# Rotary embedding on one core: VectorE work regrouped into four operations per batch, and the tables and two rows of the first batch moved to SyncE's queue in float32

## Chip, cores and metric

The kernel runs on one core of a Trainium2 chip. The metric is the device time of one execution in microseconds (us). Several executions are taken of each kernel, and a kernel under test is always timed beside the kernel before on the same chip. In the lines from the profiler, DVE is VectorE, POOL is GpSimd, ACT is ScalarE and SPq is SyncE's queue. HBM is the chip's main memory and SBUF the core's own.

## The reference

```python
x:   (8, 2048, 16, 64) float32          # batch, position, head, feature
cos, sin: (2048, 32) float32
x1, x2 = x[..., :32], x[..., 32:]
out1 = x1 * cos - x2 * sin              # cos, sin broadcast over batch and head
out2 = x1 * sin + x2 * cos
return concatenate([out1, out2], axis=-1)   # float32
```

The input is 67.1 MB and the output is 67.1 MB. Each batch is 8.39 MB of float32. The arithmetic is six operations per pair of elements, so the work is mostly moving data.

## The kernel before

Each of the 128 partitions holds J = 16 consecutive positions of one batch: 16 rows of 1024 elements. GpSimd issues every transfer. Loads convert float32 to float16 on the way in, and stores convert back. Five batch tiles are in rotation.

```python
io_pool  = tile_pool(bufs=5)
tmp_pool = tile_pool(bufs=2)
# cos_sb, sin_sb: [P, J, 32] float16

def load(b):
    xt = io_pool.tile([P, J, H, D], f16)
    nc.gpsimd.dma_start(out=xt, in_=x[b]...)          # float32 -> float16
    return xt

def tables():
    nc.gpsimd.dma_start(out=sin_sb, in_=sin...)
    nc.gpsimd.dma_start(out=cos_sb, in_=cos...)

def rotate(xt):
    for j0 in range(0, J, 8):                         # two halves of a batch
        ...                                           # js, v1, v2, x1, x2, sin_b, cos_b
        nc.vector.tensor_mul(out=v1, in0=x2, in1=sin_b)
        nc.vector.tensor_mul(out=v2, in0=x1, in1=sin_b)
        nc.vector.tensor_mul(out=xw, in0=xw, in1=cos_b)    # both halves of the features
        nc.vector.tensor_sub(out=x1, in0=x1, in1=v1)
        nc.vector.tensor_add(out=x2, in0=x2, in1=v2)

for b in range(B):
    tiles[b] = load(b)
    if b == 0:
        tables()
    if b >= 4:
        ...                                           # store b - 4
    rotate(tiles[b])
...                                                   # the last four stores
```

GpSimd issues the transfers in this order: load 0, tables, loads 1 to 4, stores 0 and 1, loads 5 and 6, stores 2 and 3, load 7, stores 4 to 7. A load that reuses a tile waits until the store from that tile has landed.

## Time and profile before

| | before |
|---|---|
| median of the first 3 executions | 318.91 us (318.77 to 319.09) |
| span of the profiled execution | 317.2 us |
| VectorE busy | 210.7 us, 66% |
| DMA queue, share of 16 engines' span | 99.6% |
| HBM traffic | 134.7 MB, 425 GB/s |

These lines are from the page of the kernel before. The rows of digits divide the span into 40 slices and give the busy share of each in tenths. The queue line gives packets, megabytes, and the packets' time as a share of 16 DMA engines' span.

```profile
span 317.2 us, 164 instructions
DVE 210.7 (66%) x80; POOL 9.9 (3%) x22
...
DVE  0009999999999999999069999995009994000000
...
DMA  7979999999999999999999999999999999999996
...
q0 software_dynamic: 2592, 100.93, 99.6%
...
HBM read 67.63 MB, written 67.11 MB: 425 GB/s over the span
```

VectorE has empty slices at the start, in the middle and at the end. The DMA row has none. The 7s near the start are an artefact: a packet is counted in the slice in which it starts, and packets here last 2.4 us and start in bunches of 16. A queue that is 99.6% busy leaves almost nothing to gain, unless the bytes, the time of a packet or the ends of the run change.

The groups of instructions (busy time in us, then mean ns of one, then the idle time before them) give the price of a VectorE operation.

```profile
L55 DVE TENSOR_TENSOR v<-xt,sin_sb 128x4096 f16<-128x4096 f16 x16 | 36.5, 2284 | 54.2 <-DMA xt<-in_x_dram 29.9
L58 DVE TENSOR_TENSOR xt<-xt,cos_sb 128x8192 f16<-128x8192 f16 x16 | 70.7, 4416 | 0.0
```

Twice the elements cost 1.93 times as much. So an operation is nearly all streaming and has only a small fixed part.

The view of waits (total us, number of waits, longest one) shows who waits for whom.

```profile
POOL xt L37 <- DMA out_dram<-xt: 118.1, 3, 56.4
POOL out_dram L68 <- DVE xt L60: 73.8, 2, 48.0
POOL out_dram L73 <- DVE xt L60: 63.0, 2, 46.2
DVE v L55 <- DMA xt<-in_x_dram: 29.9, 2, 20.2
DVE v L55 <- DMA sin_sb<-in_sin_dram: 24.3, 1, 24.3
```

GpSimd's long waits look alarming, but an issuing engine may wait as long as the DMA queue still holds work. The order of time on GpSimd shows how early the last stores are issued.

```profile
200.67 1.05 POOL L73 DMA_DIRECT2D out_dram<-xt  x2
218.56 0.53 POOL L73 DMA_DIRECT2D out_dram<-xt  x1 [16.84 <-DVE xt L60]
265.27 0.53 POOL L73 DMA_DIRECT2D out_dram<-xt  x1 [46.18 <-DVE xt L60]
```

The last store is issued at 265.3 us. By the trace's packet records its data do not start to move until 295.4. By this reading VectorE could finish the last batch almost 30 us later without any effect (an estimate).

Last, the start, in windows of 0.25 us. The columns are the window, its length, the busy time and instructions of VectorE and of GpSimd, the granted TensorE clock, and the DMA share and GB/s. These last two again go by the start of packets, so the share can exceed 1.

```profile
2.25:2.50 0.25, 0.00 (x0) 0.25 (x2) 1.00 0.00 0
2.50:2.75 0.25, 0.00 (x0) 0.25 (x1) 1.00 4.12 655
```

The DMA engines get their first data packet at 2.61 us. From there to 315.41 us the queue never runs dry.

### The profile page before, as it was taken

To read this page: it belongs to the slowest core of one execution; us is meant where nothing else is said; L and a number is where in the kernel's file an instruction comes from. 1 tells how busy PE (TensorE), PEld (TensorE's weight loads), DVE (VectorE), ACT (ScalarE), POOL (GpSimd) and SP (SyncE) were. 2 spreads that over 40 slices of the span, in tenths; PEclk is the share of its full clock that TensorE was granted. 3 is DMA by queue.
4 is the path that set the end of the run, shared out by engine and by line. 5 is a ranking of instruction groups with operands and counts; after the bars stand their busy time and mean duration, and the time that the engine had idled before them with its cause. 6 is when DMAs were issued, how large, how long until landed. Compare 5 with 4: busy or idle time off the path is not lost.

```text
span 317.2 us, 164 instructions
## 1 busy us (share of the span) xinstructions
DVE 210.7 (66%) x80; POOL 9.9 (3%) x22
## 2 busy tenths in 40 slices
DVE  0009999999999999999069999995009994000000
POOL 5000000000000000001000000100000000000000
DMA  7979999999999999999999999999999999999996
GB/s 132 256 163 266 207 198 202 260 198 198 198 264 264 397 397 529 397 331 231 231 198 199 380 413 397 454 471 264 198 314 413 397 446 479 397 397 512 413 397 264
DMA packets 2593, 100.93 MB, mean 318 GB/s; under 512 B 288, under 2 KB 544, under 8 KB 544
## 3 DMA queue, kind: packets, MB, share of 16 engines
q0 software_dynamic: 2592, 100.93, 99.6%
q14 instruction: 1, 0.01, 0.0%
HBM read 67.63 MB, written 67.11 MB: 425 GB/s over the span
## 4 chain that ended last, share of the span: by engine, by line
issue 34%; DMA 19%; DVE 16%; another core or an unknown queue 13%; POOL 1%; POOLq 0%; DVEq 0%; PEldq 0%
DMA xt<-in_x_dram 12%; DMA sin_sb<-in_sin_dram 7%; DVE xt L58 5%; DVE v L55 3%; DVE xt L60 3%; DVE v L56 3%; DVE xt L59 2%; POOL xt L37 1%; POOL out_dram L68 1%; POOLq L101 0%; POOLq L37 0%; POOLq L73 0%; DVEq L55 0%; PEldq L101 0%
## 5 line engine op out<-in xcount | busy, mean ns | idle before, releaser
L55 DVE TENSOR_TENSOR v<-xt,sin_sb 128x4096 f16<-128x4096 f16 x16 | 36.5, 2284 | 54.2 <-DMA xt<-in_x_dram 29.9
L58 DVE TENSOR_TENSOR xt<-xt,cos_sb 128x8192 f16<-128x8192 f16 x16 | 70.7, 4416 | 0.0
L59 DVE TENSOR_TENSOR xt<-xt,v 128x4096 f16<-128x4096 f16 x16 | 36.5, 2283 | 0.1
L60 DVE TENSOR_TENSOR xt<-xt,v 128x4096 f16<-128x4096 f16 x16 | 36.5, 2283 | 0.0
L56 DVE TENSOR_TENSOR v<-xt,sin_sb 128x4096 f16<-128x4096 f16 x16 | 36.5, 2283 | 0.0
L37 POOL DMA_DIRECT2D xt<-in_x_dram x8 | 4.4, 568 | 118.9 <-DMA out_dram<-xt 118.1
L68 POOL DMA_DIRECT2D out_dram<-xt x4 | 2.1, 539 | 73.8 <-DVE xt L60 73.8
L73 POOL DMA_DIRECT2D out_dram<-xt x4 | 2.1, 532 | 63.0 <-DVE xt L60 63.0
L44 POOL DMA_DIRECT2D cos_sb<-in_cos_dram x1 | 0.5, 548 | 0.0
L43 POOL DMA_DIRECT2D sin_sb<-in_sin_dram x1 | 0.5, 542 | 0.0
L90 POOL MEMSET const-float32-0.0<- 128x1 f32 x1 | 0.1, 100 | 0.2 <-issue 0.2
L90 POOL MEMSET const-bfloat16-1.0<- 128x1 bf16 x1 | 0.1, 103 | 0.0
L90 POOL MEMSET const-float32-1.0<- 128x1 f32 x1 | 0.1, 100 | 0.0
L90 POOL MEMSET const-uint8-127<- 128x1 uint8 x1 | 0.1, 100 | 0.0
## 6 DMA issues: line engine op xcount, KB each, us to landing
xt<-in_x_dram POOLq DMA_DIRECT2D x8, 4096.0 KB, 39.8
sin_sb<-in_sin_dram POOLq DMA_DIRECT2D x1, 128.0 KB, 22.2
cos_sb<-in_cos_dram POOLq DMA_DIRECT2D x1, 128.0 KB, 22.4
out_dram<-xt POOLq DMA_DIRECT2D x8, 65.9
```

The costliest lines, as they stand in the source:

```text
L37: nc.gpsimd.dma_start(out=xt, in_=x[b].rearrange("(p j) h d -> p (j h d)", j=J))
L43: nc.gpsimd.dma_start(out=sin_sb, in_=sin.rearrange("(p j) d -> p (j d)", j=J))
L44: nc.gpsimd.dma_start(out=cos_sb, in_=cos.rearrange("(p j) d -> p (j d)", j=J))
L55: nc.vector.tensor_mul(out=v1, in0=x2, in1=sin_b)
L56: nc.vector.tensor_mul(out=v2, in0=x1, in1=sin_b)
L58: nc.vector.tensor_mul(out=xw, in0=xw, in1=cos_b)
L59: nc.vector.tensor_sub(out=x1, in0=x1, in1=v1)
L60: nc.vector.tensor_add(out=x2, in0=x2, in1=v2)
L68: nc.gpsimd.dma_start(out=out[b - 4].rearrange("(p j) h d -> p (j h d)", j=J), in_=tiles[b - 4])
L73: nc.gpsimd.dma_start(out=out[b].rearrange("(p j) h d -> p (j h d)", j=J), in_=tiles[b])
L90: nc = _bacc.Bacc("TRN2", target_bir_lowering=False, num_devices=1)
```

## The change

It has two parts. The first regroups VectorE's work: the two halves of a batch are done at once, a negated sine table turns the subtraction into an addition, and a batch takes four operations in place of ten. The second lets SyncE start the first data: both tables and two of the sixteen rows of batch 0 are loaded in float32 on its queue, and ScalarE converts them to float16. (In both kernels every transfer that converts is issued by GpSimd; SyncE's are in float32.)

```diff
+    JA = 2
+    head = const_pool.tile([P, JA, H, D], f32)
+    nc.sync.dma_start(out=head..., in_=x0[:, 0:JA, :]...)
+    nc.sync.dma_start(out=sin_f, in_=sin...)          # float32 tables
+    nc.sync.dma_start(out=cos_f, in_=cos...)
     def load(b):
+        j0 = JA if b == 0 else 0
-        nc.gpsimd.dma_start(out=xt, in_=x[b]...)
+        nc.gpsimd.dma_start(out=xt[:, j0:J, :, :]..., in_=x[b]...[:, j0:J, :]...)
-    def tables(): ...                                 # two loads on GpSimd
     def rotate(xt):
-        for j0 in range(0, J, JC): ...                # five operations per half
+        nc.vector.tensor_mul(out=v[:, :, :, 0:Dh], in0=xt[:, :, :, Dh:D], in1=neg_b)
+        nc.vector.tensor_mul(out=v[:, :, :, Dh:D], in0=xt[:, :, :, 0:Dh], in1=sin_b)
+        nc.vector.tensor_mul(out=xw, in0=xw, in1=cos_b)
+        nc.vector.tensor_add(out=xa, in0=xa, in1=v...)
+    tiles = [load(b) for b in range(NBUF)]
+    nc.scalar.copy(out=tiles[0][:, 0:JA, :, :]..., in_=head...)
+    nc.scalar.copy(out=sin_h, in_=sin_f)
+    nc.scalar.mul(out=neg_h, in_=sin_f, mul=-1.0)
+    nc.scalar.copy(out=cos_h, in_=cos_f)
     for b in range(B):
         rotate(tiles[b])
+        store(b, tiles[b])
+        if b + NBUF < B:
+            tiles.append(load(b + NBUF))
```

Cuts are marked by "...". The order in which GpSimd issues loads and stores comes out the same as before, without the tables.

More of the change, by code (lines that the diff above doesn't have):

```diff
@@ L20 @@
     f16 = mybir.dt.float16
+    f32 = mybir.dt.float32
     B, S, H, D = x.shape
@@ L25 @@
     J = S // P
-    JC = 8
+    NBUF = 5
     const_pool = ctx.enter_context(tc.tile_pool(name="rope_const", bufs=1))
-    io_pool = ctx.enter_context(tc.tile_pool(name="rope_io", bufs=5))
-    tmp_pool = ctx.enter_context(tc.tile_pool(name="rope_tmp", bufs=2))
-    cos_sb = const_pool.tile([P, J, Dh], f16)
-    sin_sb = const_pool.tile([P, J, Dh], f16)
+    io_pool = ctx.enter_context(tc.tile_pool(name="rope_io", bufs=NBUF))
+    tmp_pool = ctx.enter_context(tc.tile_pool(name="rope_tmp", bufs=1))
@@ new lines @@
+    JA = 2
+    head = const_pool.tile([P, JA, H, D], f32)
+    x0 = x[0].rearrange("(p j) h d -> p j (h d)", j=J)
+    nc.sync.dma_start(
+        out=head.rearrange("p j h d -> p (j h d)"),
+        in_=x0[:, 0:JA, :].rearrange("p j f -> p (j f)"),
+    )
+    sin_f = const_pool.tile([P, J, Dh], f32)
+    cos_f = const_pool.tile([P, J, Dh], f32)
+    cos_h = const_pool.tile([P, J, Dh], f16)
+    sin_h = const_pool.tile([P, J, Dh], f16)
+    neg_h = const_pool.tile([P, J, Dh], f16)
+    nc.sync.dma_start(out=sin_f, in_=sin.rearrange("(p j) d -> p j d", j=J))
@@ L35, in load @@
+    nc.sync.dma_start(out=cos_f, in_=cos.rearrange("(p j) d -> p j d", j=J))
     def load(b):
         xt = io_pool.tile([P, J, H, D], f16)
+        j0 = JA if b == 0 else 0
         nc.gpsimd.dma_start(
-            out=xt, in_=x[b].rearrange("(p j) h d -> p (j h d)", j=J)
-        )
-        return xt
-    def tables():
-        nc.gpsimd.dma_start(out=sin_sb, in_=sin.rearrange("(p j) d -> p (j d)", j=J))
-        nc.gpsimd.dma_start(out=cos_sb, in_=cos.rearrange("(p j) d -> p (j d)", j=J))
+            out=xt[:, j0:J, :, :].rearrange("p j h d -> p (j h d)"),
+            in_=x[b].rearrange("(p j) h d -> p j (h d)", j=J)[:, j0:J, :].rearrange("p j f -> p (j f)"),
+        )
+        return xt
@@ L46, in rotate, with store @@
+    def store(b, xt):
+        nc.gpsimd.dma_start(
+            out=out[b].rearrange("(p j) h d -> p (j h d)", j=J), in_=xt
+        )
     def rotate(xt):
-        for j0 in range(0, J, JC):
-            js = slice(j0, j0 + JC)
-            v1 = tmp_pool.tile([P, JC, H, Dh], f16)
-            v2 = tmp_pool.tile([P, JC, H, Dh], f16)
-            x1 = xt[:, js, :, 0:Dh]
-            x2 = xt[:, js, :, Dh:D]
-            sin_b = sin_sb[:, js, :].unsqueeze(2).to_broadcast([P, JC, H, Dh])
-            cos_b = cos_sb[:, js, :].unsqueeze(2).to_broadcast([P, JC, 2 * H, Dh])
-            nc.vector.tensor_mul(out=v1, in0=x2, in1=sin_b)
-            nc.vector.tensor_mul(out=v2, in0=x1, in1=sin_b)
-            xw = xt[:, js, :, :].rearrange("p j h (e d) -> p j (h e) d", d=Dh)
-            nc.vector.tensor_mul(out=xw, in0=xw, in1=cos_b)
-            nc.vector.tensor_sub(out=x1, in0=x1, in1=v1)
-            nc.vector.tensor_add(out=x2, in0=x2, in1=v2)
@@ L62 @@
-    tiles = {}
-    for b in range(B):
-        tiles[b] = load(b)
-        if b == 0:
-            tables()
-        if b >= 4:
-            nc.gpsimd.dma_start(
-                out=out[b - 4].rearrange("(p j) h d -> p (j h d)", j=J), in_=tiles[b - 4]
-            )
+        v = tmp_pool.tile([P, J, H, D], f16)
+        sin_b = sin_h.unsqueeze(2).to_broadcast([P, J, H, Dh])
+        neg_b = neg_h.unsqueeze(2).to_broadcast([P, J, H, Dh])
+        cos_b = cos_h.unsqueeze(2).to_broadcast([P, J, 2 * H, Dh])
@@ new lines, in rotate @@
+        nc.vector.tensor_mul(out=v[:, :, :, 0:Dh], in0=xt[:, :, :, Dh:D], in1=neg_b)
+        nc.vector.tensor_mul(out=v[:, :, :, Dh:D], in0=xt[:, :, :, 0:Dh], in1=sin_b)
+        xw = xt.rearrange("p j h (e d) -> p j (h e) d", d=Dh)
+        nc.vector.tensor_mul(out=xw, in0=xw, in1=cos_b)
+        xa = xt.rearrange("p j h d -> p (j h d)")
+        nc.vector.tensor_add(out=xa, in0=xa, in1=v.rearrange("p j h d -> p (j h d)"))
+    tiles = [load(b) for b in range(NBUF)]
+    nc.scalar.copy(
+        out=tiles[0][:, 0:JA, :, :].rearrange("p j h d -> p (j h d)"),
+        in_=head.rearrange("p j h d -> p (j h d)"),
+    )
@@ L71 @@
+    nc.scalar.copy(out=sin_h, in_=sin_f)
+    nc.scalar.mul(out=neg_h, in_=sin_f, mul=-1.0)
+    nc.scalar.copy(out=cos_h, in_=cos_f)
+    for b in range(B):
         rotate(tiles[b])
-    for b in range(B - 4, B):
-        nc.gpsimd.dma_start(
-            out=out[b].rearrange("(p j) h d -> p (j h d)", j=J), in_=tiles[b]
-        )
+        store(b, tiles[b])
+        if b + NBUF < B:
+            tiles.append(load(b + NBUF))
 _INS = ['x', 'cos', 'sin']
```

## The prediction

> **What bounds the kernel now.** The DMA engines. The page's queue part gives the one software queue 99.6% of 16 engines' span; VectorE is busy 210.7 of 317.2 us (66%). The trace's packet records show the first data packet at 2.6 us, the last ending at 315.4, and no gap between: eight loads and eight stores, each 128 packets (8 per engine) of about 2.43 us for 64 KB of HBM data, so 19.5 us per transfer of 8.39 MB; 16 x 19.5 = 312. HBM carries 134.7 MB at 425 GB/s. The chain of waits is no guide: it calls a third of the span "issue" because transfers queue behind each other.
>
> **What the change does.**
> - VectorE: ten operations per batch become four. From the groups, 4096 elements take 2.283 us and 8192 take 4.416, so 16384 should take 8.68 (estimate). A batch is then 2 x 4.42 + 2 x 8.68 = 26.2 us, against 26.3 now (210.7 / 8): no element is saved, only fixed cost. This assumes two elements a cycle, which the Trainium skill (VectorE: DVE Perf Modes, "The perf-mode tier table") gives as the best of a 16-bit tensor-tensor operation; the 2.283 us agree (4096 / 2 / 0.96 GHz = 2.13, plus 0.15). I expect VectorE at 207 to 210 us.
> - ScalarE: four small conversions, a few us, early, off the path.
> - DMA: HBM bytes are unchanged. Two of 16 rows of batch 0 (1 MB, some 2.4 us of all engines, estimate) and the tables (1.3 us now, between landings at 23.6 and 24.8) move to another queue, still on the same 16 engines: the Trainium skill (DMA: Bandwidth & Descriptors, "Issuing engines are not separate DMA queues") says that this saves only issue time. GpSimd issues loads and stores in the same order as before.
>
> **What lies on the critical path.** Only the start. Engines are released at 0.84 us, data flows from 2.6, and the first round of packets takes 2.9 to 3.4 us in place of 2.43. SyncE may get data moving some tenths of a us earlier and fill part of the slow first round: 0 to 1.5 us, about 0.8. The end (last store landing at 315.7, span ending 1.5 later) is unchanged.
>
> VectorE's slack hides the rest: store 0 is issued at 53 us but moves only from 102; store 7 is issued at 265 and moves from about 296. Even if SyncE's small packets take turns one for one with the 64 KB packets, so that VectorE starts at 42 instead of 24, batch 0 is ready by 69.
>
> **Prediction.** 318.1 us (before: 318.91); 8 in 10 between 316.9 and 319.2. Faster by over 2%: 0.01; within 2%: 0.98; slower by over 2%: 0.01.
>
> **What would show it right or wrong.**
> - Queue part: software queue near 98 to 99%, a new hardware queue near 1%; HBM bytes as before.
> - Groups: two operations of 4.4 and two of 8.7 us per batch. About 8.6 and 17.2 would mean the fast mode is lost: VectorE, near 410 us, would be the bound.
> - Packet records: first data at 1.8 to 2.6 us; 19.3 to 19.5 us between landings; last store landing 0 to 1.5 us earlier.
> - Stores issued before the queue runs dry.
>
> **What would make it wrong.** Two queues costing the engines efficiency while both are active (at most the first 20 to 40 us); first data no earlier; a longer launch with two more engines in use; the fast mode lost with the strided output of the sine products.

## The result and the profile after

| | before | after |
|---|---|---|
| median of 6 executions | 319.03 us (318.77 to 319.15) | 317.86 us (317.65 to 317.96) |
| ratio after / before | | 0.9963, 95% interval 0.995 to 0.9976 |
| span of the profiled execution | 317.2 us | 316.1 us |
| VectorE busy | 210.7 us | 209.2 us |
| first data packet | 2.61 us | 1.74 us |
| last data packet ends | 315.41 us | 314.27 us |

The change is worth 1.2 us, or 0.4%, and lies within 2%.

The page of the changed kernel:

```profile
span 316.1 us, 121 instructions
...
DVE 209.2 (66%) x32; ACT 4.9 (2%) x5; POOL 8.8 (3%) x20
...
DVE  0009799999999999999879999990009993000000
...
DMA  9899999999999999999999999999999999999996
...
q0 software_dynamic: 2304, 100.14, 98.5%
q1 hardware_dynamic: 432, 1.57, 1.4%
HBM read 67.63 MB, written 67.11 MB: 426 GB/s over the span
```

HBM bytes are the same to the last digit shown. A hardware queue (SyncE's) has appeared with 1.4%, and the two queues' shares add up to 99.9%. The DMA engines are as full as they were.

The groups:

```profile
L70 DVE TENSOR_TENSOR xt<-xt,cos_h 128x16384 f16<-128x16384 f16 x8 | 69.5, 8692 | 2.0 <-ACT cos_h L81 1.7
L67 DVE TENSOR_TENSOR v<-xt,neg_h 128x8192 f16<-128x8192 f16 x8 | 35.4, 4426 | 52.2 <-DMA xt<-in_x_dram 52.0
L72 DVE TENSOR_TENSOR xt<-xt,v 128x16384 f16<-128x16384 f16 x8 | 69.5, 8692 | 0.3
L68 DVE TENSOR_TENSOR v<-xt,sin_h 128x8192 f16<-128x8192 f16 x8 | 35.4, 4419 | 0.0
```

Four operations do the work of ten in the same time: 48 operations less have saved 1.5 us of VectorE's 210.7, and VectorE idles as before.

The waits:

```profile
POOL out_dram L58 <- DVE xt L72: 136.3, 4, 50.5
POOL xt L51 <- DMA out_dram<-xt: 118.3, 3, 56.4
DVE v L67 <- DMA xt<-in_x_dram: 52.0, 3, 24.8
ACT cos_h L81 <- DMA cos_f<-in_cos_dram: 17.7, 1, 17.7
...
DVE xt L70 <- ACT cos_h L81: 1.7, 1, 1.7
```

GpSimd's two sums are what they were (136.3 against 73.8 + 63.0, and 118.3 against 118.1). One new wait has come: the cosine table arrives late. The table of DMA issues (KB, then us from issue to landing) shows how late:

```profile
head<-in_x_dram SPq DMA_DIRECT2D x1, 1024.0 KB, 4.8
sin_f<-in_sin_dram SPq DMA_DIRECT2D x1, 256.0 KB, 13.4
cos_f<-in_cos_dram SPq DMA_DIRECT2D x1, 256.0 KB, 31.8
```

The tables are small, but a table packet is one row of 2 KB. The packet records suggest that each DMA engine takes about one such packet, then one 57 KB packet of batch 0 (2.13 us), and so on in turns: from 7.4 to 20.5 us, 80 table packets start in six rounds of 16 large packets. VectorE loses 1.7 us to it and has the slack to lose it.

The last stores on GpSimd:

```profile
199.55 1.05 POOL L58 DMA_DIRECT2D out_dram<-xt  x2
212.86 0.53 POOL L58 DMA_DIRECT2D out_dram<-xt  x1 [12.25 <-DVE xt L72]
263.88 0.53 POOL L58 DMA_DIRECT2D out_dram<-xt  x1 [50.50 <-DVE xt L72]
```

The last store is issued 1.4 us earlier, close to the size of the whole gain. That suggests a rival explanation, which the experiments test. The start, in the same windows (there is now a column for ScalarE):

```profile
1.50:1.75 0.25, 0.00 (x0) 0.25 (x1) 0.25 (x1) 1.00 0.51 66
1.75:2.00 0.25, 0.00 (x0) 0.25 (x1) 0.25 (x2) 1.00 1.74 295
```

Data flow from 1.74 us, which is 0.87 us earlier than before. SyncE began to issue at 0.74 us and its first packet came 1.00 us later. GpSimd began at 1.25 in both kernels, and its first packet came 1.36 us later in the kernel before. So 0.51 us is the earlier issue and 0.36 the shorter time from issue to first packet.

### The profile page after: what moved, and what is told of

Its sections match the earlier page's. It is cut to its first block, busy times and chain, and to the rows that moved or that the text cites. A ratio compares the mean times of both kernels' runs of the same rounds, so it can differ in the third digit from the quotient of the medians.

```text
span 316.1 us, 121 instructions
## 1 busy us (share of the span) xinstructions
DVE 209.2 (66%) x32; ACT 4.9 (2%) x5; POOL 8.8 (3%) x20
## 3 DMA queue, kind: packets, MB, share of 16 engines
q0 software_dynamic: 2304, 100.14, 98.5%
## 4 chain that ended last, share of the span: by engine, by line
issue 44%; DVE 14%; another core or an unknown queue 14%; DMA 10%; POOL 1%; SPq 0%; ACT 0%; POOLq 0%
DMA cos_f<-in_cos_dram 10%; DVE xt L70 6%; DVE xt L72 6%; DVE v L67 1%; DVE v L68 1%; POOL out_dram L58 1%; POOL xt L51 0%; ACT cos_h L81 0%; POOLq L112 0%; SPq L45 0%; SPq L36 0%; POOLq L58 0%
## 5 line engine op out<-in xcount | busy, mean ns | idle before, releaser
L70 DVE TENSOR_TENSOR xt<-xt,cos_h 128x16384 f16<-128x16384 f16 x8 | 69.5, 8692 | 2.0 <-ACT cos_h L81 1.7
L67 DVE TENSOR_TENSOR v<-xt,neg_h 128x8192 f16<-128x8192 f16 x8 | 35.4, 4426 | 52.2 <-DMA xt<-in_x_dram 52.0
L72 DVE TENSOR_TENSOR xt<-xt,v 128x16384 f16<-128x16384 f16 x8 | 69.5, 8692 | 0.3
L68 DVE TENSOR_TENSOR v<-xt,sin_h 128x8192 f16<-128x8192 f16 x8 | 35.4, 4419 | 0.0
L58 POOL DMA_DIRECT2D out_dram<-xt x8 | 4.3, 535 | 136.3 <-DVE xt L72 136.3
L51 POOL DMA_DIRECT2D xt<-in_x_dram x8 | 4.4, 559 | 119.1 <-DMA out_dram<-xt 118.3
L75 ACT CAST xt<-head 128x2048 f16<-128x2048 f32 x1 | 1.9, 1897 | 3.5 <-DMA head<-in_x_dram 3.5
## 6 DMA issues: line engine op xcount, KB each, us to landing
cos_f<-in_cos_dram SPq DMA_DIRECT2D x1, 256.0 KB, 31.8
```

Source lines behind the costliest of these rows:

```text
L51: nc.gpsimd.dma_start(out=xt[:, j0:J, :, :].rearrange("p j h d -> p (j h d)"), in_=x[b].rearrange("(p j) h d -> p j (h d)", j=J)[:, j0:J, ...
L58: nc.gpsimd.dma_start(out=out[b].rearrange("(p j) h d -> p (j h d)", j=J), in_=xt)
L67: nc.vector.tensor_mul(out=v[:, :, :, 0:Dh], in0=xt[:, :, :, Dh:D], in1=neg_b)
L68: nc.vector.tensor_mul(out=v[:, :, :, Dh:D], in0=xt[:, :, :, 0:Dh], in1=sin_b)
L72: nc.vector.tensor_add(out=xa, in0=xa, in1=v.rearrange("p j h d -> p (j h d)"))
L75: nc.scalar.copy(out=tiles[0][:, 0:JA, :, :].rearrange("p j h d -> p (j h d)"), in_=head.rearrange("p j h d -> p (j h d)"),)
```

## The experiments

Theory A: the DMA engines are the bound from first to last packet, and the gain is that their first packet comes earlier. Rivals: B, VectorE's shorter chain brings the last store forward; C, the amount of data moved to SyncE counts; D, taking the small table packets out of GpSimd's queue counts; E, the form without conversion counts.

**How the packet records are read here.** Every DMA engine goes through 128 large packets in a row, 8 of each of 16 transfers, each about 2.41 us after the last (2.2 us where batch 0 has 57 KB rows). The records do not name the engine, so packets are chained here by their times: the next one starts where one ends. That gives 16 chains, an inference but a stable one, since from store 0 on they keep their places to 0.06 us except for an instruction fetch told below (and except in e8, whose queue runs dry). The time of the last data packet's end is then a sum of three terms: when the median chain starts its last packet, how far the latest chain is behind the median ("the straggler"), and 2.45 us for the last packet. For the kernel before that is 312.49 + 0.47 + 2.45 = 315.41 us. All values are of the profiled execution, one per kernel.

| kernel | first data packet | median chain, last packet starts | straggler | last data packet ends | time, median (range) | ratio to before, 95% interval |
|---|---|---|---|---|---|---|
| before | 2.61 | 312.49 | 0.47 | 315.41 | 319.03 (318.77 to 319.15) | |
| after | 1.74 | 311.50 | 0.32 | 314.27 | 317.86 (317.65 to 317.96) | 0.9963 (0.995 to 0.9976) |
| e1_vector_only | 2.62 | 312.32 | 0.31 | 315.09 | 318.67 (318.59 to 318.69) | 0.9988 (0.9976 to 1.0) |
| e2_sync_only | 1.76 | 311.53 | 0.46 | 314.44 | 317.98 (317.93 to 318.46) | 0.997 (0.9958 to 0.9981) |
| e3_tables_on_sync | 1.75 | 311.68 | 0.47 | 314.60 | 318.57 (317.98 to 320.16) | 0.9995 (0.9974 to 1.0017) |
| e4_head_on_sync | 1.74 | 311.71 | 0.45 | 314.61 | 318.33 (318.21 to 318.6) | 0.9979 (0.9966 to 0.9992) |
| e5_same_on_gpsimd | 2.64 | 312.32 | 0.58 | 315.35 | 318.99 (318.87 to 319.51) | 1.0006 (0.9992 to 1.0019) |
| e6_tables_late | 2.62 | 312.31 | 0.74 | 315.50 | 319.1 (318.92 to 319.28) | 1.0006 (0.9993 to 1.0018) |
| e7_one_more_op | 1.75 | 311.46 | 1.21 | 315.12 | 318.57 (317.92 to 318.83) | 0.9984 (0.9972 to 0.9997) |
| e8_two_more_ops | 1.74 | 323.85 | 0.43 | 326.73 | 330.39 (329.79 to 330.46) | 1.0356 (1.0342 to 1.037) |
| e9_early_store | 1.74 | 311.75 | 0.32 | 314.51 | 318.08 (317.86 to 318.19) | 0.9972 (0.996 to 0.9983) |
| e10_head_1 | 1.73 | 311.34 | 1.04 | 314.83 | 318.34 (317.72 to 318.81) | 0.9979 (0.9967 to 0.9991) |
| e11_tables_again | 1.75 | 311.84 | 1.77 | 316.07 | 319.68 (318.58 to 321.28) | 1.0027 (1.0001 to 1.0052) |
| e12_tiny_ops | 1.73 | 311.85 | 0.50 | 314.80 | 317.79 (317.71 to 318.34) | 0.9964 (0.995 to 0.9977) |

The third column sorts the kernels, e8 apart, into two groups with nothing between: 312.31 to 312.49 where GpSimd sends the first packet at 2.6 us, and 311.34 to 311.85 where SyncE sends it at 1.7. Each value is from one execution.

### e1_vector_only: the first part alone

```diff
 # to the kernel before
-        five operations on each half, tmp bufs=2
+        the four operations of the change, tmp bufs=1
+        nc.scalar.mul(out=neg_sb, in_=sin_sb, mul=-1.0)
```

> Only the four-operation VectorE form; the tables stay float16 on GpSimd's queue behind the first load, and no data moves on SyncE. Theory A (the gain is the earlier first data packet on a saturated DMA): same as before, 319.0 us, ratio 0.9995 to 1.0005; first packet at 2.6 us; VectorE busy about 209 us. Rival B (the gain comes from VectorE's shorter chain, which issues the last store 1.4 us earlier): the whole gain, 317.9 us, ratio about 0.9963.

It took 318.67 us, ratio 0.9988. Rival B is refuted: its 0.9963 lies outside the interval. VectorE was busy 209.2 us as in the changed kernel and the last store was issued at 264.7, but the time hardly moved. The 0.4 us that did appear is more than theory A allowed (0.9995), though the interval ends at 1.0.

### e2_sync_only: the second part alone

```diff
 # to the kernel after
-        the four operations, tmp bufs=1
+        five operations on each half, tmp bufs=2
-    nc.scalar.mul(out=neg_h, in_=sin_f, mul=-1.0)
```

> Only the SyncE part (two rows of batch 0 and both tables in float32 on SyncE, ScalarE casts); VectorE keeps its ten operations per batch. Theory A: the whole gain, 317.9 us, ratio 0.996 to 0.997; first packet at about 1.74 us. Rival B: no gain, 319.0 us, ratio about 1.000.

It took 317.98 us, ratio 0.997, with the first packet at 1.76 us. Nearly all of the gain is in this part, as theory A said, while VectorE still does ten operations per batch.

### e3_tables_on_sync, and again as e11_tables_again

```diff
 # to the kernel before
+    nc.sync.dma_start(out=sin_f, in_=sin...)          # float32
+    nc.sync.dma_start(out=cos_f, in_=cos...)
     def tables():
-        nc.gpsimd.dma_start(out=sin_sb, in_=sin...)
-        nc.gpsimd.dma_start(out=cos_sb, in_=cos...)
+        nc.scalar.copy(out=sin_sb, in_=sin_f)
+        nc.scalar.copy(out=cos_sb, in_=cos_f)
```

> Only the tables in float32 on SyncE; batch 0 is loaded whole by GpSimd, VectorE keeps ten operations. Theory A: first packet at about 1.74 us; the tables are 16 packets of some 0.08 us per engine, 1.3 us in all, enough to fill the 0.87 us before GpSimd's first packet, so most of the gain: 317.9 to 318.3 us, ratio 0.9965 to 0.9978. Rival C (the head's two rows are what counts, since only they are large): 318.8 us or more, ratio above 0.999. Rival B: 1.000.

> The kernel with only the tables on SyncE once more, on what may be another chip, since its first six times fell in two groups (three at 318.0 to 318.1 us, three at 319.0 to 320.2). Theory A says that its start is worth 1.15 us, as its first profile shows at the start of the second load, so most times at 318.0 to 318.3 us, ratio 0.9965 to 0.998. If it is slower in itself: again half of the times above 319 us.

Both miss what theory A expected. The first six times were 318.12, 317.98, 318.11, 319.01, 320.16 and 319.98. On another chip they were 318.58 to 321.28, slower than the kernel before. So the alternatives came instead: e3's ratio is above rival C's 0.999 (its median is a little under rival C's 318.8), and in e11 more than half of the times are above 319 us. Yet in both profiled executions the first packet came at 1.75 us, and the median chain was early: 311.68 and 311.84. In e11 one chain was 1.77 us behind the median at the end, and already 1.46 behind at its second packet, 7.6 us into the run: the straggler spent the gain. The profiled execution of e3 was one of its fast ones (318.12), so that a straggler made its slow ones slow is likely but not shown. The records thus bear out theory A for the DMA engines as a whole, but the time is set by the last of 16. Rival C stays open: by the times, the kernel without the two rows gained nothing clear of noise; by the records, its median chain was about as early as with them.

### e4_head_on_sync: only the two rows

```diff
 # to the kernel before
+    nc.sync.dma_start(out=head..., in_=x0[:, 0:2, :]...)      # float32
     load 0: rows 2 to 15 on GpSimd
+    nc.scalar.copy(out=tiles[0][:, 0:2, :, :]..., in_=head...)
```

> Only the two rows of batch 0 in float32 on SyncE; the tables stay float16 on GpSimd's queue, VectorE keeps ten operations. Theory A: first packet at about 1.74 us and most of the gain, 317.9 to 318.3 us, ratio 0.9963 to 0.9978. Rival D (the gain is from taking the small table packets out of GpSimd's queue): no gain, 319.0 us, ratio about 1.000.

It took 318.33 us, ratio 0.9979, a hair outside what theory A expected (up to 318.3 and 0.9978). Rival D is refuted as the main cause: the tables still sit in GpSimd's queue, and 0.7 us of the gain are there.

### e5_same_on_gpsimd: the same pieces, the other queue

```diff
 # to the kernel after
-    nc.sync.dma_start(...)       # head, sin_f, cos_f
+    nc.gpsimd.dma_start(...)
```

> The changed kernel, with the two rows of batch 0 and the two tables still in float32 and still first, but issued by GpSimd on its one queue. Theory A (what counts is SyncE's earlier first packet): first packet at about 2.6 us again, and at most the part of the gain that the VectorE form showed alone (0.4 us): 318.6 to 319.1 us, ratio 0.9985 to 1.0005. Rival E (what counts is the float32 form without a cast, or small first packets): 317.9 us, ratio about 0.9965.

It took 318.99 us, ratio 1.0006: the gain is gone. Rival E is refuted. The kernel has the four-operation VectorE form too, and the 0.4 us of e1 do not show here (the interval goes down to 0.9992). The windows of this kernel show the first packet back in the same place as before the change:

```profile
2.25:2.50 0.25, 0.00 (x0) 0.00 (x0) 0.25 (x2) 1.00 0.00 0
2.50:2.75 0.25, 0.00 (x0) 0.00 (x0) 0.25 (x1) 1.00 1.09 197
```

This is the cleanest single test: the same bytes in the same pieces in the same order, and only the issuing engine differs. It leaves one rival: with SyncE come both the earlier first packet and a second queue beside GpSimd's, and no run has one without the other. So that the second queue itself adds to the gain is not ruled out.

The trace of e3 shows where time is won. In the kernel before, the tables delay load 1 by about 1.3 us (its median chain starts load 1 at 24.23 us, and at 22.89 in e6, where the tables come later). In e3 all table packets start between 1.75 and 3.64 us, and the median chain starts its second large packet at 6.10 us, against 6.00 in the kernel before. The tables cost the loads 0.1 us there, since they ran before and during GpSimd's slow first packets.

### e6_tables_late: VectorE starts 39 us later

```diff
 # to the kernel before
-        if b == 0:
+        if b == 2:
             tables()
+            rotate(tiles[0])
+            rotate(tiles[1])
-        rotate(tiles[b])
+        if b >= 2:
+            rotate(tiles[b])
```

> The kernel before, with the table loads queued behind the third load, so that VectorE starts at about 64 us in place of 24. Theory A (VectorE has slack: batch 0 would be ready at about 90 us and its store's data move from 102): no change, 318.8 to 319.3 us, ratio 0.999 to 1.001. If VectorE's chain sets the time: up to 40 us later, 340 us or more.

It took 319.1 us, ratio 1.0006, as expected. These lines are from its page and its view of waits:

```profile
DVE  0000000099999999999999999999999999400000
...
DVE v L55 <- DMA sin_sb<-in_sin_dram: 62.9, 1, 62.9
```

VectorE sat still for 62.9 us in place of 24.3 and then ran almost without a pause. The time did not notice.

### e7_one_more_op and e8_two_more_ops: how much slack

```diff
 # to the kernel after; once more in e7, twice more in e8
         nc.vector.tensor_mul(out=v[:, :, :, Dh:D], in0=xt[:, :, :, 0:Dh], in1=sin_b)
+        nc.vector.tensor_mul(out=v[:, :, :, Dh:D], in0=xt[:, :, :, 0:Dh], in1=sin_b)
```

> The changed kernel with one sine product done twice: 4.42 us more VectorE time per batch, 35 us in all. Theory A: by the queue's order the last batch is ready at about 270 us and its store's data move from 294.6, so no change: 317.7 to 318.1 us, ratio to before 0.9957 to 0.9972, though VectorE is then busy 245 us. If VectorE's chain (rival B) counted at all, the last store comes some 6 us later and so does the end, 324 us.

> The changed kernel with one sine product done three times: 8.84 us more per batch, 71 us in all. By Theory A's model of the queue VectorE now runs without a wait from 24 us, the last batch is ready at about 304 us, 9 to 10 us after the queue has run dry at 294.6, and the time rises by 9 to 12 us: 327 to 330 us, ratio to before 1.025 to 1.035.

The busy times of e7 and of e8:

```profile
DVE 244.6 (77%) x40; ACT 4.9 (2%) x5; POOL 8.9 (3%) x20
DVE 280.0 (85%) x48; ACT 4.9 (2%) x5; POOL 8.9 (3%) x20
```

e7 had VectorE busy 244.6 us and took 318.57 us, 0.5 more than expected. Its executions spread from 317.92 to 318.83. In the profiled one (318.82) the median chain is where the changed kernel has it (311.46 against 311.50), and one straggler is 1.21 us late. The latest chain was 0.94 behind already at its second packet, some 16 us before VectorE's first operation. So in that execution most of the lateness is not VectorE's doing, and rival B's 324 us did not come. The other slow executions were not profiled.

e8 took 330.39 us, 11.4 more than the 319.02 of the kernel before in the same rounds and 12.5 more than the changed kernel's 317.86 of other rounds. The expected 327 to 330 us are 9 to 12 above the changed kernel, so the rise, the time and the ratio are all a little above their ranges. Its last store on GpSimd and its row of DMA slices:

```profile
305.82 0.53 POOL L58 DMA_DIRECT2D out_dram<-xt  x1 [34.63 <-DVE xt L74]
```

```profile
DMA  9999989999899999899998999989999899970896
```

Store 7 is issued at 305.8 us, after the queue ran dry, and the DMA row has a zero in it for the first time. Here is the limit: about 245 us of VectorE work are free in this kernel, and 280 are not.

### e9_early_store: a stall where loads turn to stores

The records of all kernels show one more loss of the size discussed here: the last packets before store 0 (about 98 us into the run) mostly take 2.5 to 3.9 us in place of 2.43, on average 2.80 before and 3.37 after.

```diff
 # to the kernel after, behind the load of head
+    nc.sync.dma_start(out=out[0]...[:, 0, 0:D], in_=head[:, 0, 0, :])   # store 0 overwrites it
```

> The changed kernel with one more, tiny transfer: SyncE stores 256 bytes per partition into batch 0's output as soon as its two rows have landed (store 0 overwrites them later, so the result stays right). The trace of both kernels shows the last packets before the first store stretched to 2.8 to 3.4 us in place of 2.43, and no later store does that. Theory F (the first write to the output costs that once): the stall moves to the early store, the packets before store 0 take about 2.43 us, and the time falls by 0.3 to 0.9 us to 317.0 to 317.6, ratio to before 0.993 to 0.9955. If the stall belongs to the turn from loads to stores: no change, 317.9 us, 0.9965.

It took 318.08 us, ratio 0.9972, and the packets before store 0 still took 3.41 us. Theory F is refuted. What causes the stall stays open. Its size differs from kernel to kernel (on average 2.68 us a packet in e10, 3.79 in e12; one execution each), and it blurs the comparison: the median chain's lead over the kernel before was 1.20 us at the start of load 1, 1.43 at load 4 and 0.94 at store 0. So in the changed kernel's profiled execution the stall took back about 0.5 us; whether that belongs to the change is not shown.

### e10_head_1: one row in place of two

```diff
 # to the kernel after
-    JA = 2
+    JA = 1
```

> The changed kernel with one row of batch 0 on SyncE in place of two: 0.5 MB, some 1.2 us of all engines. Theory A: one row still covers the 0.87 us before GpSimd's first packet, so the same gain: 317.8 to 318.2 us, ratio 0.996 to 0.9975. Rival C (the amount moved to SyncE counts): half of the gain, 318.4 us, ratio about 0.998.

The median of 318.34 us (317.72 to 318.81) and the ratio of 0.9979 are where rival C put them and just outside theory A's range (up to 318.2 and 0.9975), but the interval reaches into both. The records of the one profiled execution do not decide either. At the end the median chain was as early as with two rows (311.34), with a straggler of 1.04 us. But at the start of load 2, when the tables had landed, it led the kernel before by only 0.52 us, against 1.02 with two rows; it caught up in a shorter stall before store 0 (2.68 us a packet on average in place of 3.37). Against rival C stands e3: it moves the fewest bytes on SyncE and led by 1.22 us at the same point. Whether the amount counts stays open.

### e12_tiny_ops: as many instructions as before

In every kernel with 80 VectorE instructions, one 8 KB packet of the instruction queue falls in the run, at 169 to 172 us (201 in e6, where VectorE is late). In the kernel before it moves one chain back by 0.54 us. With 32 instructions there is none.

```diff
 # to the kernel after
+        for _ in range(6):
+            nc.vector.tensor_add(out=xa[:, 0:2], in0=xa[:, 0:2], in1=tiny)   # tiny is zero
```

> The changed kernel with 48 two-element VectorE additions of zero (six per batch), which bring VectorE's instructions from 32 to 81, as many as before; the result is unchanged. Theory G (the small gain of the VectorE form alone is that its shorter program needs no instruction fetch in the middle of the run; with 80 instructions one 8 KB fetch packet comes at about 170 us and holds one DMA engine up by 0.5 us, 0.2 us of it at the end): the fetch packet is back in the trace at 160 to 180 us and the last data packet ends 0 to 0.5 us later than in the changed kernel; time 317.8 to 318.4 us. If the instruction count does nothing: no fetch packet after the start, 317.6 to 318.0 us.

The packet is back, at 169.4 us, and the last data packet ended 0.53 us later than in the changed kernel in the one profiled execution, the slowest of the five. Of this, 0.35 is the median chain, which was already 0.3 late at store 0, before the fetch, and 0.18 the straggler. The median time is 317.79 us, ratio 0.9964, which is the changed kernel's. So the instruction count brings the fetch, as theory G said, but no cost that the times resolve. The 0.4 us of e1 therefore stay without a shown cause.

No experiment beat the changed kernel by more than the spread of its own executions.

## Why the prediction was right

- **The bound.** Right. Both kernels fill 16 DMA engines (99.6%, then 98.5 + 1.4%) with the same HBM bytes. e6, e7 and e8 show VectorE's slack directly.
- **VectorE.** Right. The predicted 4.42 and 8.68 us measured 4.42 and 8.69. The prediction's 2.13 us for 4096 elements is an estimate with the clock of 0.96 GHz that the page it names, the Trainium skill's "VectorE: DVE Perf Modes", gives under "Specifications"; the trace agrees, since 4096 further elements took 2.13 us (4.416 - 2.284), which leaves 0.15 fixed. The predicted 207 to 210 us measured 209.2. The predicted effect on the time was none; alone it gave 0.4 us with an interval that reaches zero (e1), and in e5 nothing.
- **The start.** Right in kind. The predicted gain was 0 to 1.5 us, about 0.8; it measured 1.2. The first packet came at 1.74 us, a little before the predicted 1.8 to 2.6. Of the 1.14 us between the last packets' ends, 0.99 is the median chain and 0.15 the straggler. By the start of load 1 the lead was 1.20 us, of which 0.87 is the earlier first packet. The other 0.33 includes the slow first round (GpSimd's first packets took 3.12 us before and 2.14 after, of a full 2.43 and 2.13), which the prediction had named, and the tables, and is not separated. How near the size came is partly luck: the stall before store 0 took back about 0.5 us, and SyncE's pieces alone gave between nothing by the ratio (e3, e11) and 0.7 us (e4).
- **Packets taking turns.** The prediction named it as a risk without effect, and it came: the cosine table landed at 33.5 us, VectorE waited 1.7 us, and the time did not care.
- **The end.** Right. The last store landed at 314.63 in place of 315.75 us, 1.12 earlier, and the span ended about 1.5 us after it both times.
- **What it did not see.** The time is set by the latest of 16 DMA engines, and in the profiled executions with a large straggler (e7, e10, e11) one chain was late by its second packet. That may be why e3, e10 and e11 scatter by about as much as the effect or more; their other executions were not profiled.

## What to carry to other kernels

When the DMA queue is full from the first packet to the last, look first at the two ends: how soon the first data packet leaves, and whether the queue ever runs dry. Faster arithmetic is worth nothing while the stores are issued ahead of the queue, and slower arithmetic costs nothing until they are not. When differences are below 1%, look at the latest DMA engine as well as the total: in e11 the lead of all engines was spent by one that fell behind in the first microseconds.

## What the Trainium skill lacked or had wrong

- "DMA: Bandwidth & Descriptors", "Issuing engines are not separate DMA queues": it says that issuing from several engines saves only the sequencer's issue time, usually small. The runs agree that it is small, but here it is more than issue time: 0.51 us of earlier issue plus 0.36 us less from issue to first packet (1.00 against 1.36 us). The page's "Specifications" do have such a difference, about 1 against 0.6 us to the first byte. What the section lacks is that in a kernel whose DMA engines are full to the end, such a lead can reach the total: after 0.87 us of earlier data the time fell by 1.2 us.
- "DMA: Bandwidth & Descriptors", "Where 436 GB/s comes from": it calls the SBUF ports the bottleneck. In these converting transfers 65,536 bytes of HBM data take 2.412 us from packet to packet, which is 434.7 GB/s over 16 engines and fits the page's 435.2. But the SBUF side carries only half of those bytes, in float16. The page does not say which side paces a converting transfer. Here the rate fits the float32 side; that is also the HBM side, and no run separates the two.
- "DMA: Bandwidth & Descriptors", "Queues, rings and completion order": it gives packets of 9 to 17 descriptors as typical before an engine changes queues. In the changed kernel each engine seems to have changed after about one 2 KB row, against one 57 KB row of the other queue (80 table rows in six rounds of 16 engines; the records do not name the engine), and a 256 KB table took 31.8 us to land.
- No page that we read has the stall where loads turn to stores: mostly 2.5 to 3.9 us for a packet of 2.43, once per run; e9's profiled execution shows that an earlier small write does not remove it.
- "DMA: Bandwidth & Descriptors", "Latency and other measured facts": it names two engines as usually slower. The records do not name the engine, so no run shows whether the straggler is one of them. The page does not say that a delay from the first two rounds can last to the end: in the profiled executions the latest chain ended 0.31 to 1.77 us behind the median, and 1.46 of the largest were there at its second packet. What holds that engine up stays open.
